# WKV recurrence of an RWKV layer on one core: quarter-array matmuls, four stores a pair, split rows for w and u, zero matmuls in pauses

## The chip, the core and the metric

The kernel runs on one core of a Trainium2 chip. The metric is the device time of one execution in microseconds; before the change the median of three runs is 369.63 us (368.87 to 372.65). The engines are named as in the profile: PE (TensorE; PEld is its weight load), DVE (VectorE), ACT (ScalarE), POOL (GpSimd) and SP (SyncE, which here only issues transfers).

## What is computed

The inputs are k and v (16 sequences of 2,048 steps by 256 channels, f32) and two vectors of 256, w and u. Each sequence and channel has a running numerator, a running denominator and a running maximum:

```python
for t in range(seq_len):
    ww = u + kk
    qq = np.maximum(pp, ww)
    e1 = np.exp(pp - qq); e2 = np.exp(ww - qq)
    output[b, t, :] = (e1 * aa + e2 * vv) / (e1 * bb + e2 + 1e-08)
    ww = pp - w + kk
    qq = np.maximum(ww, kk)
    e1 = np.exp(ww - qq); e2 = np.exp(kk - qq)
    aa = e1 * aa + e2 * vv
    bb = e1 * bb + e2
    pp = qq
```

So every step is weighted by exp(k), a state decays by exp(-w) a step, and the current step has the bonus u.

## The kernel before

**Tiling.** Time is cut into 16 chunks of 128 steps, each of two halves of 64 (`HS`). The 16 sequences are taken four at a time. One such piece (128 steps x 4 sequences x 256 channels, 512 KB) is called a pair in the code, numbered n = 4 * chunk + group; there are 64. On the chip the 128 steps are the partitions, and a tile has 128 x 1024 elements, seen as [128, 2, 512].

**One pair.** `load_k` and `load_v` (lines 61 and 66) bring 512 KB each. `round_k` (164) casts k for TensorE on DVE. `logs` (178) forms two exponents in the four PSUM banks of X: a small matmul of rows of w and u (tile `WU`, one or two rows at partitions 0, 32, 64 and 96) with coefficients `CO`, then a matmul of k with `NLE` or `NLZ`. `exps` (190) takes exp on ACT into the bf16 ring `EZR` (12 pairs). `cast_v` (197) makes v bf16, `times_v` (202) multiplies on DVE, so the ring holds four quarters: two for the denominator (0 and 1), two for the numerator (2 and 3). Ten pairs later (`LAG`) `den` (317) sums along time: matrix L (lower triangle with ones, zero between the two halves) times quarter 0, plus the identity times quarter 1, over the full 128 x 128 array, two column halves of 512 each: four matmuls of 128x512. `num` (331) does the same with LN and IdN. `recip` (325) forms 1/den on ACT as exp(-ln). `mult` (338) multiplies on DVE and stores the pair with one transfer of 512 KB from SP.

**The state.** Once a chunk, `sums` (224; 32 matmuls of 32 columns by 256), `copy_sums`, `turn` (242), `copy_turn`, `state_logs`, `state_shift`, `state_frames`, `state_offsets`, `state_weights`, `state_chain`, `state_spread`, `turn_back` (297) and `inject` (303) carry the states of all 16 sequences from half to half on PE, DVE, ACT and POOL. `inject` writes the states into rows 63 and 127 of the chunk's ring entries with four small transfers of 8 KB, so that den and num pick them up. den of a chunk's first pair needs them.

**Order.** The order is written out by hand: `keep_in_program_order` fixes it, and the loop from line 370 is one slot n per turn (76 slots). In a slot: exps(n), mult(n-11), logs(n+1), round_k(n+2), recip(n-10), den(n-9), num(n-10), times_v(n), cast_v(n+1), loads. The dictionary `later` (344) places each state step at a slot and at a place in it. Loads are issued from SP for the first 16 pairs and from POOL after that; stores and, from the third chunk on, the rows of `inject` come from SP. X takes four PSUM banks, den two and num two, each with one buffer; `num`'s banks also serve the state's matmuls. In the first nine pairs (`HALVES`) den's banks are a third buffer for the exponents (`X2`).

Of the kernel before, what the change touches and what calls it, by code (L numbers as in the profile page):

```python
# [7 lines left out]
F32 = mybir.dt.float32  # L8
F32R = mybir.dt.float32r
BF16 = mybir.dt.bfloat16  # L10
ALU = mybir.AluOpType
# [4 lines left out]
def kernel(  # L16
# [9 lines left out]
    K = tc.keep_in_program_order  # L26
    PE, DVE, SC, POOL, SP = nc.tensor, nc.vector, nc.scalar, nc.gpsimd, nc.sync

    B, T, Dm = k.shape
    HS = 64  # L30
    TC = 2 * HS
    NST = T // TC
    D = 2 * Dm
    NP = 4 * NST
    RING = 12
    LAG = 10
    FIRST = 16
    HALVES = 9
# [5 lines left out]
    consts = ctx.enter_context(tc.tile_pool(name="consts", bufs=1))  # L44
# [7 lines left out]
    psd = ctx.enter_context(tc.tile_pool(name="psd", bufs=1, space=bass.MemoryType.PSUM))  # L52
# [4 lines left out]
    def rows_of(x, n):  # L57
        c, p = divmod(n, 4)
        return x[4 * p:4 * p + 4, c * TC:(c + 1) * TC, :].rearrange("n t d -> t n d")

    def load_k(n, q):
        kr = kpool.tile([128, 4, Dm], F32, tag="kr", name="kr")
        K(q.dma_start(out=kr, in_=rows_of(k, n)))  # L63
        kr_of[n] = kr

    def load_v(n, q):
        vr = vpool.tile([128, 4, Dm], F32, tag="vr", name="vr")
        K(q.dma_start(out=vr, in_=rows_of(v, n)))  # L68
        vr_of[n] = vr


    wuf = consts.tile([128, 2, Dm], F32, tag="wuf", name="wuf")

    def rows_wu(q, x, g0):
        q = K(q.dma_start(out=wuf[g0::32, :, :], in_=bass.AP(
            tensor=x.tensor, offset=x.offset, ap=[[0, (128 - g0 + 31) // 32], [0, 2], list(x.ap[0])])))

    rows_wu(SC, w, 0)
    load_k(0, SP)
    rows_wu(SP, u, 65)  # L80
    load_k(1, SP)
    for n in range(NBUF - 1):
        load_v(n, SP)
# [3 lines left out]
    Z = consts.tile([128, D], BF16, tag="Z", name="Z")  # L87
# [9 lines left out]
    GE, NE = ALU.is_ge, ALU.not_equal  # L97

    def select(ap, cmp, fill, base, cm, pattern):
        K(POOL.affine_select(out=ap, in_=ap, pattern=pattern, compare_op=cmp,  # L100
                             fill=fill, base=base, channel_multiplier=cm))

    def matrix(name, dt):
        return consts.tile([128, 128], dt, tag=name, name=name)
# [6 lines left out]
    COf = matrix("COf", F32)  # L111
    for h in range(2):
        K(POOL.iota(COf[HS * h:HS * h + HS, :], pattern=[[0, 2], [1, HS]], base=-HS // 2 - h, channel_multiplier=0,
                    allow_small_or_imprecise_dtypes=True))
    for g in (2, 3):
        select(COf, NE, 1.0, -32 * g - 1, 1, [[0, 128]])

    NLE, NLZ, CO = matrix("NLE", F32R), matrix("NLZ", F32R), matrix("CO", F32R)
    K(DVE.tensor_scalar(NLE, M1, 0.5, None, ALU.add))
    for h in range(2):  # L120
        fill(NLE[HS * h:HS * h + HS, HS * (1 - h):HS * (2 - h)], 0.0)
    K(DVE.tensor_tensor(NLZ, NLE, I1, ALU.add))
    K(DVE.tensor_copy(CO, COf))
    WU = consts.tile([128, D], F32R, tag="WU", name="WU")
    for g, r in ((0, 1), (32, 1), (64, 2), (96, 2)):
        K(DVE.tensor_copy(WU[g:g + r, :], wuf[g:g + r].rearrange("p n d -> p (n d)")))

    mats = {}

# [30 lines left out]
    def ez(n):  # L160
        return EZR[:, :, n % RING]
# [5 lines left out]
        KM[n] = km  # L167

    X = psx.tile([128, 2, 2, D], F32, tag="X", name="X")
    X2 = psd.tile([128, 2, D], F32, tag="den", name="X2")  # L170

    def part_of(n, q):
        if n >= HALVES:
            return X[:, q]
        j = (2 * n + q) % 3
        return X2 if j == 2 else X[:, j]

    def logs(n, qs=(0, 1)):
        km = KM[n].rearrange("p (i n) d -> p i (n d)", i=2)
        for q in qs:  # L180
            for i in range(2):
                g = 32 * (2 * q + i)
                K(PE.matmul(part_of(n, q)[:, i, :], CO[g:g + 1 + q, :], WU[g:g + 1 + q, :], start=True, stop=False,  # L183
                            tile_position=(g, 0), skip_group_check=True))
        for q in qs:
            for i in range(2):
                K(PE.matmul(part_of(n, q)[:, i, :], (NLE, NLZ)[q], km[:, i, :], start=False, stop=True,  # L187
                            skip_group_check=True))
# [8 lines left out]
    def cast_v(n, eng):  # L197
        vb = vbpool.tile([128, 4, Dm], BF16, tag="vb", name="vb")
        K(eng.tensor_copy(vb, vr_of.pop(n)))  # L199
        VB[n] = vb  # L200

    def times_v(n):
        vb = VB.pop(n).rearrange("p (i n) d -> p i (n d)", i=2)
        K(DVE.tensor_mul(ez(n)[:, 2:4], ez(n)[:, 0:2], vb.unsqueeze(1).broadcast_to([128, 2, 2, D])))  # L204
# [98 lines left out]
    def inject(c):  # L303
        cb = small.tile([128, 128], BF16, tag="cb", name="cb")
        K(DVE.tensor_copy(cb, st.pop((c, "CT"))))  # L305
        r0 = 4 * c % RING
        for q in (1, 0):
            for h in range(2):
                r, x = HS * h + HS - 1, 32 * (2 * q + h)
                K((POOL if c < 2 else SP).dma_start(  # L310
                    out=EZR[r:r + 1, 2 * (1 - q), r0:r0 + 4, :, :].rearrange("o p i (b x) -> o (p i b) x", b=4),
                    in_=cb[x:x + 32, :]))


    DEN, RD, NUM = {}, {}, {}

    def den(n):
        d = psd.tile([128, 2, D], F32, tag="den", name="den")
        for m, q in (("L", 0), ("Id", 1)):
            for i in range(2):  # L320
                K(PE.matmul(d[:, i, :], mats[m], ez(n)[:, q, i, :], start=q == 0, stop=q == 1,  # L321
                            skip_group_check=True))
        DEN[n] = d

    def recip(n):
        rd = rpool.tile([128, 2, D], F32, tag="rd", name="rd")
        K(SC.activation(rd, DEN.pop(n), ACT.Ln, scale=RS))  # L327
        K(SC.activation(rd, rd, ACT.Exp, scale=-1.0))  # L328
        RD[n] = rd

    def num(n):
        d = psn.tile([128, 2, D], F32, tag="num", name="num")
        for m, q in (("LN", 2), ("IdN", 3)):
            for i in range(2):
                K(PE.matmul(d[:, i, :], mats[m], ez(n)[:, q, i, :], start=q == 2, stop=q == 3, skip_group_check=True))  # L335
        NUM[n] = d

    def mult(n):
        o = opool.tile([128, 4, Dm], F32, tag="ot", name="ot")
        K(DVE.tensor_mul(o.rearrange("p (i n) d -> p i (n d)", i=2), NUM.pop(n), RD.pop(n)))  # L340
        K(SP.dma_start(out=rows_of(out, n), in_=o))

    later = {}
    for c in range(NST):
        s = 4 * c + 3
        for slot, where, f in ((s + 1, "pe", sums), (s + 1, "dve", copy_sums),
                               (s + 2, "pe", turn), (s + 2, "dve", copy_turn),
                               (s + 3, "act", state_logs), (s + 3, "act", state_shift), (s + 3, "dve0", state_frames),
                               (s + 3, "dve0", state_offsets),
                               (s + 4, "act", state_weights), (s + 4, "dve", state_chain), (s + 4, "dve", state_spread),  # L350
                               (s + 4, "pe1", turn_back), (s + 4, "dve1", inject),
                               (s + 4, "end", state_keep)):
            later.setdefault((slot, where), []).append((f, c))

    def small_work(n, where):
        for f, c in later.pop((n, where), []):
            f(c)

    round_k(0)
    logs(0, (0,))  # L360
    logs(0, (1,))
    load_k(NBUF, SP)
    load_v(NBUF - 1, SP)
# [6 lines left out]
    for n in range(NP + LAG + 2):  # L370
        q = n - LAG
        if n < NP:
            exps(n)
        small_work(n, "act")
        if 0 <= q - 1 < NP:
            mult(q - 1)
        if n + 1 < HALVES:
            logs(n + 1, (0,))
            logs(n + 1, (1,))
        elif n + 1 < NP:  # L380
            logs(n + 1)
        small_work(n, "dve0")
        if n + 2 < NP:
            round_k(n + 2)
        small_work(n, "pe")
        small_work(n, "dve")
        if 0 <= q < NP:
            recip(q)
        if 0 <= q + 1 < NP:
            den(q + 1)  # L390
        small_work(n, "pe1")
        small_work(n, "dve1")
        if 0 <= q < NP:
            num(q)
        if n < NP:
            times_v(n)
        if n + 1 < NP:
            cast_v(n + 1, DVE if n < LAG else POOL)
        m = n + 1 + NBUF
        if m + 1 < NP:  # L400
            load_k(m + 1, SP if m + 1 < FIRST else POOL)
        if m < NP:
            load_v(m, SP if m < FIRST else POOL)
        small_work(n, "end")
        if n == 2:
            out_matrices()
# [32 lines left out]
```

## Time and profile before

| | |
|---|---|
| runs | 372.65, 368.87, 369.63 us |
| profiled execution | 367.2 us, span 365.5 us |
| mean granted clock of TensorE | 0.844 |
| busy: PE, DVE, ACT, POOL | 304.1, 257.4, 257.6, 196.3 us |
| HBM read, written | 67.12 MB, 33.55 MB |
| exp of a pair (ACT L195, 128x2048) | 1.87 us |
| ln and exp for 1/den (ACT L327, L328) | 1.02 and 1.06 us |
| cast of k, product with v, final product (DVE L166, L204, L340) | 0.87, 1.24, 1.22 us |
| issue of a k load, a v load on POOL (L63, L68) | 0.83, 0.83 us |
| issue of a store on SP (L341), of a row transfer on SP (L310) | 0.37, 0.54 us |
| store, from issue to landing | 5.4 us median, 2.9 to 10.6 |
| from one final product (DVE L340) to the next, between 60 and 290 us | 3.8 to 7.5 us |

In the profile the span is cut into 40 slices of 9.1 us; a digit is the busy share of a slice in tenths. PEclk is the granted clock of TensorE in tenths. DMA is the mean busy share of the 16 DMA engines. Stages between two times give busy time by engine, and in the timeline each line has its start, its length and what released it. A line number names the place in the kernel.

### The profile page before, as it was taken

What the parts mean: (1) busy time and instruction counts of PE and PEld (TensorE: products, weight loads), DVE (VectorE), ACT (ScalarE), POOL (GpSimd) and SP (SyncE); (2) the same over time, 40 slices, a digit from 0 to 9 for tenths busy, and PEclk for the clock granted to TensorE, in tenths of its full rate; (3) what the DMA queues carried; (4) which work ended last, traced back from release to release, by engine and by line L of the source; (5) the groups of instructions that cost most, each with busy time, mean ns of one, the idle gap of its engine ahead of it and who ended that gap; (6) DMA issues with size and microseconds to landing.
All of it is one profiled execution on the core that took longest, in us unless ns stands there. A gap on an engine that the chain in (4) does not pass through costs nothing.

```text
span 365.5 us, 4884 instructions
## 1 busy us (share of the span) xinstructions
PE 304.1 (83%) x1674; PEld 143.6 (39%) x1674; DVE 257.4 (70%) x355; ACT 257.6 (70%) x234; POOL 196.3 (54%) x279
## 2 busy tenths in 40 slices
PE   7789797969799696987989697988969788976682
PEld 2335353535344243443435253444425343533230
DVE  4773867878857757588866887575686889883652
ACT  1553558879758677679768797576775789993782
POOL 2700457887837738477764677575465745250100
PEclk9556658999859679699958997695887999998997
DMA  7999998899998979989998999889797995242465
GB/s 222 354 348 348 351 341 254 281 372 300 355 314 246 316 238 319 298 255 318 336 318 256 344 315 352 284 275 296 257 317 244 324 308 177 77 159 95 143 223 179
DMA packets 67498, 101.52 MB, mean 278 GB/s; under 512 B 5894, under 2 KB 55186, under 8 KB 67474
## 3 DMA queue, kind: packets, MB, share of 16 engines
q0 software_dynamic: 14080, 50.40, 43.2%
q1 hardware_dynamic: 53382, 50.80, 42.2%
q8 instruction: 13, 0.21, 0.2%
q14 instruction: 11, 0.09, 0.1%
q10 hardware_dynamic: 12, 0.01, 0.0%
HBM read 67.12 MB, written 33.55 MB: 275 GB/s over the span
## 4 chain that ended last, share of the span: by engine, by line
PE 62%; DVE 20%; POOL 6%; ACT 5%; issue 3%; DMA 2%; SPq 0%; DVEq 0%; POOLq 0%; ACTq 0%
PE X L187 17%; PE num L335 15%; PE den L321 13%; PE X L183 7%; DVE ot L340 7%; PE tot L231 6%; DVE km L166 4%; DVE EZR L204 4%; ACT rd L327 3%; PE TS L246 2%; PE CT L300 2%; DVE AB L284 2%; DMA vr<-in_v_dram 2%; ACT EZR L193 2%; POOL U L271 2%
## 5 line engine op out<-in xcount | busy, mean ns | idle before, releaser
L195 ACT ACTIVATE EZR<-X 128x2048 bf16<-128x2048 f32 x55 | 102.7, 1868 | 32.3 <-PE X L187 32.3
L340 DVE TENSOR_TENSOR ot<-num,rd 128x1024 f32<-128x1024 f32 x64 | 78.2, 1222 | 30.5 <-ACT rd L327 10.5
L199 POOL CAST vb<-vr 128x1024 bf16<-128x1024 f32 x53 | 55.0, 1038 | 83.1 <-DVE EZR L204 83.1
L204 DVE TENSOR_TENSOR EZR<-EZR,vb 128x2048 bf16<-128x2048 bf16 x64 | 79.5, 1241 | 2.1 <-ACT EZR L193 1.9
L327 ACT ACTIVATE rd<-den 128x1024 f32<-128x1024 f32 x64 | 65.1, 1017 | 16.6 <-PE den L321 13.9
L328 ACT ACTIVATE rd<-rd 128x1024 f32<-128x1024 f32 x64 | 67.8, 1059 | 2.0
L321 PE MATMUL den<-EZR,L 128*128 128x512 bf16 x128 | 42.4, 416 | 22.6 <-ACT rd L327 22.2
L166 DVE CAST km<-kr 128x1024 fp32r<-128x1024 f32 x64 | 55.5, 867 | 2.4 <-PE X L187 1.9
L187 PE MATMUL X<-km,NLE 128*128 128x512 f32 x128 | 54.1, 508 | 1.8 <-DVE km L166 0.9
L183 PE MATMUL X<-WU,CO 1*128 1x512 f32 (+1 forms) x256 | 42.8, 563 | 10.0 <-ACT EZR L195 5.8
L335 PE MATMUL num<-EZR,LN 128*128 128x512 bf16 x128 | 41.9, 412 | 8.7 <-DVE cb L305 5.7
L187 PE MATMUL X<-km,NLZ 128*128 128x512 f32 x128 | 47.8, 459 | 0.0
L68 POOL DMA_DIRECT2D vr<-in_v_dram x48 | 40.0, 832 | 5.0 <-DVE vb L199 4.2
L321 PE MATMUL den<-EZR,Id 128*128 128x512 bf16 x128 | 41.4, 407 | 0.0
L335 PE MATMUL num<-EZR,IdN 128*128 128x512 bf16 x128 | 41.3, 406 | 0.0
L63 POOL DMA_DIRECT2D kr<-in_k_dram x48 | 39.9, 830 | 0.0
L183 PEld LDWEIGHTS X<-WU,CO 1*128 1x128 f32 (+1 forms) x256 | 15.9, 205 | 47.2 <-issue 16.6
L193 ACT ACTIVATE EZR<-X 128x1024 bf16<-128x1024 f32 x18 | 17.9, 1022 | 20.2 <-PE X L187 20.1
L187 PEld LDWEIGHTS X<-km,NLZ 128*128 128x128 f32 x128 | 27.1, 219 | 9.2 <-issue 3.4
L187 PEld LDWEIGHTS X<-km,NLE 128*128 128x128 f32 x128 | 22.0, 215 | 20.3 <-issue 16.1
L239 DVE COPY ts<-tot 128x256 f32<-128x256 f32 x16 | 6.8, 425 | 32.2 <-PE tot L231 32.2
L231 PE MATMUL tot<-EZR,OH 128*32 128x256 bf16 x512 | 25.3, 364 | 1.4 <-DVE ot L340 1.4
(60 smaller groups left out, 233.3 us busy)
## 6 DMA issues: line engine op xcount, KB each, us to landing
out_dram<-ot SPq DMA_DIRECT2D x64, 512.0 KB, 5.4
kr<-in_k_dram POOLq DMA_DIRECT2D x48, 512.0 KB, 6.2
vr<-in_v_dram POOLq DMA_DIRECT2D x48, 512.0 KB, 7.3
kr<-in_k_dram SPq DMA_DIRECT2D x16, 512.0 KB, 8.8
vr<-in_v_dram SPq DMA_DIRECT2D x16, 512.0 KB, 8.7
EZR<-cb SPq DMA_DIRECT2D x56, 8.0 KB, 4.6
EZR<-cb POOLq DMA_DIRECT2D x8, 8.0 KB, 5.0
wuf<-in_w_dram ACTq DMA_DIRECT2D x1, 8.0 KB
```

The lines of the kernel that those rows point to most:

```text
L166: K(DVE.tensor_copy(km, kr_of.pop(n)))
L183: K(PE.matmul(part_of(n, q)[:, i, :], CO[g:g + 1 + q, :], WU[g:g + 1 + q, :], start=True, stop=False, tile_position=(g, 0), skip_group_che ...
L187: K(PE.matmul(part_of(n, q)[:, i, :], (NLE, NLZ)[q], km[:, i, :], start=False, stop=True, skip_group_check=True))
L195: K(SC.activation(ez(n)[:, 0:2], X, ACT.Exp))
L199: K(eng.tensor_copy(vb, vr_of.pop(n)))
L204: K(DVE.tensor_mul(ez(n)[:, 2:4], ez(n)[:, 0:2], vb.unsqueeze(1).broadcast_to([128, 2, 2, D])))
L231: K(PE.matmul(t[32 * j:32 * j + 32, :], mats["OH"][:, s:s + 32], ez(4 * c + p)[:, 2 * q, i, 256 * x:256 * x + 256], start=p == 0 and x == ...
L321: K(PE.matmul(d[:, i, :], mats[m], ez(n)[:, q, i, :], start=q == 0, stop=q == 1, skip_group_check=True))
L327: K(SC.activation(rd, DEN.pop(n), ACT.Ln, scale=RS))
L328: K(SC.activation(rd, rd, ACT.Exp, scale=-1.0))
L335: K(PE.matmul(d[:, i, :], mats[m], ez(n)[:, q, i, :], start=q == 2, stop=q == 3, skip_group_check=True))
L340: K(DVE.tensor_mul(o.rearrange("p (i n) d -> p i (n d)", i=2), NUM.pop(n), RD.pop(n)))
```

## The change

- `den` and `num` no longer use the full array. The function `quarters` gives, for each of the two matrices, four matmuls of 64x64 by 512: one for each time half h and each column half i, at array position (64 h, 64 i). The result has another layout: partitions are 64 i + step, and the two banks are the time halves.
- So a pair's output tile holds two sequences along the partitions, and `mult` stores it with four transfers of 128 KB, one for each h and b; on the memory side each is [2 sequences, 64 steps, 256].
- w and u go to TensorE as two bf16 rows each (`WH`, and `WU` = the value less its bf16 part where `part` is -1); `CO` is bf16. Four transfers, two on ACT and two on POOL, load w and u after a memset of `wuf`.
- State steps stand elsewhere: `sums` and `turn` come before `logs` in their slot, the state's DVE chain before `round_k`, `state_logs` and `state_weights` a slot earlier and after `recip`, `turn_back` and `inject` before `den`. `times_v` comes before `num`.
- `keep_going` adds matmuls of zeros (128x512): into den's banks, six a slot in seven of the first nine slots; after that three or six a slot, accumulated onto the next den, up to slot 62. They number 288. `X2` is gone.
- k is always loaded from SP; v from POOL from pair 16 on, as before. Of `inject`'s four rows two go from POOL and two from SP.

```diff
-    rows_wu(SC, w, 0)
     load_k(0, SP)
-    rows_wu(SP, u, 65)
+    rows_wu(SC, w, 0)
+    rows_wu(SC, w, 1)
+    rows_wu(POOL, u, 66)
+    rows_wu(POOL, u, 67)
...
-                K((POOL if c < 2 else SP).dma_start(
+                K((POOL if q == 1 else SP).dma_start(
...
-        for m, q in (("L", 0), ("Id", 1)):
-            for i in range(2):
-                K(PE.matmul(d[:, i, :], mats[m], ez(n)[:, q, i, :], start=q == 0, stop=q == 1,
-                            skip_group_check=True))
+        quarters(d, n, (("L", 0), ("Id", 1)))
         DEN[n] = d
+
+    def quarters(d, n, parts):
+        for m, q in parts:
+            for h in range(2):
+                for i in range(2):
+                    r, x = HS * h, HS * i
+                    K(PE.matmul(d[x:x + HS, h, :], mats[m][r:r + HS, r:r + HS], ez(n)[r:r + HS, q, i, :],
+                                start=q == parts[0][1], stop=q == parts[1][1], tile_position=(r, x),
+                                skip_group_check=True))
+
+    def keep_going(d, count, first):
+        for j in range(count):
+            K(PE.matmul(d[:, j % 2, :], Z[:, 0:128], Z, start=first, stop=True, skip_group_check=True))
...
-        K(DVE.tensor_mul(o.rearrange("p (i n) d -> p i (n d)", i=2), NUM.pop(n), RD.pop(n)))
-        K(SP.dma_start(out=rows_of(out, n), in_=o))
+        K(DVE.tensor_mul(o.rearrange("p (h n) d -> p h (n d)", h=2), NUM.pop(n), RD.pop(n)))
+        c, p = divmod(n, 4)
+        for h in range(2):
+            for b in range(2):
+                K(SP.dma_start(out=bass.AP(tensor=out.tensor,
+                                           offset=out.offset + ((4 * p + b) * T + c * TC + h * HS) * Dm,
+                                           ap=[[2 * T * Dm, 2], [Dm, HS], [1, Dm]]),
+                               in_=o[:, 2 * h + b, :]))
...
+        if q + 1 < 0:
+            idle_den(0 if n % 4 == 3 else 6)
+        elif n + 1 < NP:
+            keep_going(DEN[q + 1], 3 if n % 4 in (0, 3) else 6, False)
         if n + 1 < NP:
             cast_v(n + 1, DVE if n < LAG else POOL)
+        small_work(n, "pool1")
         m = n + 1 + NBUF
-        if m + 1 < NP:
-            load_k(m + 1, SP if m + 1 < FIRST else POOL)
         if m < NP:
             load_v(m, SP if m < FIRST else POOL)
+        if m + 1 < NP:
+            load_k(m + 1, SP)
```

More of the change, by code (lines that the diff above doesn't have):

```diff
@@ L72 @@
     wuf = consts.tile([128, 2, Dm], F32, tag="wuf", name="wuf")
+    K(DVE.memset(wuf, 0.0))
     def rows_wu(q, x, g0):
@@ L76, in rows_wu @@
             tensor=x.tensor, offset=x.offset, ap=[[0, (128 - g0 + 31) // 32], [0, 2], list(x.ap[0])])))
+    load_k(0, SP)
     rows_wu(SC, w, 0)
-    load_k(0, SP)
-    rows_wu(SP, u, 65)
+    rows_wu(SC, w, 1)
+    rows_wu(POOL, u, 66)
+    rows_wu(POOL, u, 67)
     load_k(1, SP)
@@ L114 @@
                     allow_small_or_imprecise_dtypes=True))
-    for g in (2, 3):
-        select(COf, NE, 1.0, -32 * g - 1, 1, [[0, 128]])
-    NLE, NLZ, CO = matrix("NLE", F32R), matrix("NLZ", F32R), matrix("CO", F32R)
+    for r in (66, 67, 98, 99):
+        select(COf, NE, 1.0, -r, 1, [[0, 128]])
+    part = consts.tile([128, 1], F32, tag="part", name="part")
+    K(POOL.memset(part, 0.0))
+    for r in (1, 33, 65, 97, 67, 99):
+        select(part, NE, -1.0, -r, 1, [[0, 1]])
+    NLE, NLZ, CO = matrix("NLE", F32R), matrix("NLZ", F32R), matrix("CO", BF16)
     K(DVE.tensor_scalar(NLE, M1, 0.5, None, ALU.add))
@@ L123 @@
     K(DVE.tensor_copy(CO, COf))
-    WU = consts.tile([128, D], F32R, tag="WU", name="WU")
-    for g, r in ((0, 1), (32, 1), (64, 2), (96, 2)):
-        K(DVE.tensor_copy(WU[g:g + r, :], wuf[g:g + r].rearrange("p n d -> p (n d)")))
+    WH = consts.tile([128, D], BF16, tag="WH", name="WH")
+    WU = consts.tile([128, D], BF16, tag="WU", name="WU")
+    wul = wuf.rearrange("p n d -> p (n d)")
+    K(DVE.tensor_copy(WH, wul))
+    K(DVE.scalar_tensor_tensor(WU, WH, part, wul, op0=ALU.mult, op1=ALU.add))
     mats = {}
@@ L169 @@
     X = psx.tile([128, 2, 2, D], F32, tag="X", name="X")
-    X2 = psd.tile([128, 2, D], F32, tag="den", name="X2")
     def part_of(n, q):
[L173 to L176, printed above, removed]
+        return X[:, q]
     def logs(n, qs=(0, 1)):
@@ L182, in logs @@
                 g = 32 * (2 * q + i)
-                K(PE.matmul(part_of(n, q)[:, i, :], CO[g:g + 1 + q, :], WU[g:g + 1 + q, :], start=True, stop=False,
+                K(PE.matmul(part_of(n, q)[:, i, :], CO[g:g + 2 + 2 * q, :], WU[g:g + 2 + 2 * q, :], start=True, stop=False,
                             tile_position=(g, 0), skip_group_check=True))
@@ L332, in num @@
         d = psn.tile([128, 2, D], F32, tag="num", name="num")
-        for m, q in (("LN", 2), ("IdN", 3)):
-            for i in range(2):
-                K(PE.matmul(d[:, i, :], mats[m], ez(n)[:, q, i, :], start=q == 2, stop=q == 3, skip_group_check=True))
+        quarters(d, n, (("LN", 2), ("IdN", 3)))
         NUM[n] = d
@@ L345 @@
         s = 4 * c + 3
[L346 to L351, printed above, removed]
+        for slot, where, f in ((s + 1, "pe0", sums), (s + 1, "dve3", copy_sums),
+                               (s + 2, "pe0", turn), (s + 2, "dve1", copy_turn),
+                               (s + 2, "act", state_logs), (s + 2, "pool1", state_shift),
+                               (s + 3, "dve0", state_frames), (s + 3, "dve0", state_offsets),
+                               (s + 3, "act", state_weights),
+                               (s + 4, "dve0", state_chain), (s + 4, "dve0", state_spread),
+                               (s + 4, "pe1", turn_back), (s + 4, "dve2", inject),
                                (s + 4, "end", state_keep)):
@@ L357, in small_work, with idle_den @@
             f(c)
+    def idle_den(count):
+        if count:
+            keep_going(psd.tile([128, 2, D], F32, tag="den", name="den"), count, True)
     round_k(0)
@@ L373 @@
             exps(n)
-        small_work(n, "act")
         if 0 <= q - 1 < NP:
             mult(q - 1)
+        small_work(n, "pe0")
+        small_work(n, "dve0")
         if n + 1 < HALVES:
@@ L381 @@
             logs(n + 1)
-        small_work(n, "dve0")
         if n + 2 < NP:
             round_k(n + 2)
-        small_work(n, "pe")
-        small_work(n, "dve")
+        small_work(n, "dve1")
         if 0 <= q < NP:
             recip(q)
+        small_work(n, "act")
+        small_work(n, "pe1")
+        small_work(n, "dve2")
         if 0 <= q + 1 < NP:
             den(q + 1)
-        small_work(n, "pe1")
-        small_work(n, "dve1")
+        if n < NP:
+            times_v(n)
+        small_work(n, "dve3")
         if 0 <= q < NP:
             num(q)
-        if n < NP:
-            times_v(n)
+        if q + 1 < 0:
+            idle_den(0 if n % 4 == 3 else 6)
+        elif n + 1 < NP:
+            keep_going(DEN[q + 1], 3 if n % 4 in (0, 3) else 6, False)
         if n + 1 < NP:
             cast_v(n + 1, DVE if n < LAG else POOL)
+        small_work(n, "pool1")
         m = n + 1 + NBUF
-        if m + 1 < NP:
-            load_k(m + 1, SP if m + 1 < FIRST else POOL)
         if m < NP:
             load_v(m, SP if m < FIRST else POOL)
+        if m + 1 < NP:
+            load_k(m + 1, SP)
         small_work(n, "end")
```

## The prediction

> **What bounds the kernel now.** I read the slices first, then the stages between times, the timeline of one slot, and last the DMA queues with their packet counts.
>
> ```profile
> PEclk9556658999859679699958997695887999998997
> DMA  7999998899998979989998999889797995242465
> GB/s 222 354 348 348 351 341 254 281 372 300 355 314 246 316 238 319 298 255 318 336 318 256 344 315 352 284 275 296 257 317 244 324 308 177 77 159 95 143 223 179
> ```
>
> The clock of TensorE falls to half again and again, yet the DMA engines are eight to nine tenths busy until the loads end at about 300 us. Two stretches of four slots each (one chunk) show what the clock does:
>
> ```profile
> 204.00:222.80 18.80, 15.61 (x106) 7.83 (x105) 15.45 (x22) 15.88 (x14) 13.90 (x19) 1.00 1.00 330
> 244.90:267.90 23.00, 19.77 (x106) 9.25 (x105) 15.34 (x22) 15.88 (x14) 13.63 (x19) 0.78 0.88 273
> ```
>
> The columns are length, busy us of PE, PEld, DVE, ACT, POOL, then clock, DMA share and GB/s. The same work takes 18.80 us at the full clock and 23.00 at 0.78. At the full clock the DMA share is 1.00: the engines of the chip are balanced, and DMA is the next limit at once. In the timeline of one slot at the full clock:
>
> ```profile
> 301.62 0.59 PE L321 MATMUL den<-EZR,L 128*128 128x512 bf16 x2
> 302.05 0.59 PE L321 MATMUL den<-EZR,Id 128*128 128x512 bf16 x2
> 302.49 0.59 PE L335 MATMUL num<-EZR,LN 128*128 128x512 bf16 x2
> 314.28 1.06 PE L231 MATMUL tot<-EZR,OH 128*32 128x256 bf16 x32
> ```
>
> Two matmuls start every 0.43 us, 0.215 each. The last line has 32 matmuls of 256 columns in 1.06 us, 33 ns each where one alone streams for 107: column tiles do run beside each other, 3.2 of 4. The queues:
>
> ```profile
> DMA packets 67498, 101.52 MB, mean 278 GB/s; under 512 B 5894, under 2 KB 55186, under 8 KB 67474
> q0 software_dynamic: 14080, 50.40, 43.2%
> q1 hardware_dynamic: 53382, 50.80, 42.2%
> q10 hardware_dynamic: 12, 0.01, 0.0%
> ```
>
> These counts tell over how many engines a transfer is spread. On q1 run 96 transfers of 512 rows of 1 KB, 56 of 32 rows of 256 B, and u's one of 4 rows: 50,948 rows. The count is 53,382, so 2,434 are extra: 152 x 16 + 2. Queue q10 is w's one transfer: 8 rows, 12 packets, 4 extra. The small packets agree: 5,894 less the 1,792 rows of 256 B is 4,102 = 2,434 + 4 + 104 x 16 (q0's). So a transfer whose outermost count is 128 or 32 has 16 extra packets, w's (4 partitions) 4, and u's (2 partitions) 2: one for each engine taking part, and the outermost count caps the engines.
>
> **The change part by part.** The profiled execution took 367.2 us, its span 365.5, so 1.7 lie around; the median shown is 369.63, 2.4 above. Sums are against 367.2.
>
> *Stores (decides).* Today a store is 128 rows outermost on both sides, 16 engines, 512 KB, landing in 5.4 us. After, four stores of 128 KB have 128 partitions on the on-chip side but [2, 64, 256] on the memory side: outermost count 2, as in u's transfer. Bounds: 16 engines each (nothing changes), or two engines, the same two each time. No row has the counts 128 and 2 together. I take two, because both sides must be cut alike and u's is the only row with a count of 2; and the same two, because u's and w's rows show nothing that would move a later transfer on. Then these two engines carry 4 x 64 = 256 rows of 1 KB per pair, and their sixteenth of k and v, 64 KB. Price of one KB: 348 to 354 GB/s in the first slices over 16 engines is 46.8 ns; the best slice, 372, gives 44.0; q1's whole share (42.2% of 16 x 365.5 us for 50.80 MB) 49.7. I take 45.4, midway of the first two, since two engines have the memory nearly to themselves. Stores: 64 x 256 x 45.4 ns = 744 us. Loads still to come when the first store issues at 60 us: the first 6.5 slices of 9.1 us move 19 MB of the 67.1 read, so 48 MB, a sixteenth is 2,930 KB, 133 us. Sum: 60 + 744 + 133 + 3 for the last landing + 1.7 + 1 (head, below) = 943 us. At 44.0 it is 916, at 49.7 about 1,026.
>
> [...] By the row of today's stores alone, 16 engines, the sum would be that of the first rival.
>
> *SP's queue.* Per slot it held one store and one transfer of a state row into EZR; now four stores, one k load and half a row transfer. An EZR transfer takes 0.54 us to issue, a store 0.37: at most 4 x 0.54 + 0.44 + 0.27 = 2.9 us per slot, under the 5.2 of a slot. In the built program each of SP's transfers waits on a semaphore of the eighth before it; that was four slots, now 1.45. Behind a late store stand the k load and the row into EZR, for which den of the next chunk waits on PE. With two engines this only keeps about two pairs of stores queued, so the two engines stay busy: no price beyond the sum. With 16 engines, 1.45 slots are 6.8 us against 5.4 to land: covered by 1.4.
>
> *Quarters.* den and num lose 8 matmuls of 0.215 (1.72 us) and get 16 of 64x64, four places of the array. Bounds: all four at once 0.86, one by one 3.44. I take 1.08, by the 3.2 of 4 of the tot row: -0.64 us a slot on PE.
>
> *Zeros.* 288 matmuls of 128x512, 246 of them in 54 slots: 4.6 x 0.215 = 0.98 us per slot on PE, standing before the next CO and km matmuls, which ACT's exp waits for. Zeros do hold the clock: the ten at the start (1.26 to 5.7 us) leave the first slice at 9 tenths. Bounds -0.5 to +0.98 a slot: with the clock held, a chunk of 20.7 (mult's starts at 58.4 and 307.0, twelve chunks apart) becomes 18.8, -0.5; I take -0.5 where PE sets the pace, and nothing behind the stores.
>
> *State work moved to the front of a slot and a slot earlier.* The waits it aims at are ACT G on POOL U, 26.8 us in 15, and den on ACT rd, 22.2 in 16. At most both go, 49 us; DVE's state chain now stands ahead of its km cast, which could cost its 1.4 us x 16. I take -15, inside what DMA leaves. *k loads from POOL to SP:* POOL loses 48 x 0.83 us and gains 24 EZR issues of 0.6, off the path; EZR's q=1 half leaves SP. *w and u in two bf16 parts:* CO loads fall from 205 towards 105 ns, hidden; 0 to -0.1 a slot, 0 taken. *Head:* w and u in four transfers behind a memset, ten more small POOL operations of about 0.3 us, so WU comes 0 to 2 us later than at 6.46: +1; DMA share is 1.10 there and covers most.
>
> All parts but the stores: 12 chunks from 20.7 to what DMA allows, 6.3 MB at 350 GB/s = 17.9, is -34, plus the head: 334.
>
> **The rivals.**
> 1. *Faster: the four stores go over all engines* (or another two each time). Then DMA stays at 4.5 us a slot, and the gain above stands: 334 us, 320 at 372 GB/s, 350 if only the clock's half comes. For it: every large transfer so far used 16. Against it: u's 2 extra packets. It decides from the engine count k: per pair (512 KB / k) x 45.4 ns + 2.9 equals today's 5.2 at k = 10.
> 2. *Quarters one after the other.* 3.44 + 0.98 against 1.72 adds 2.7 us to a PE slot of 3.8, 6.5 against 5.2: about 450 us, with stores spread. Against it: the tot row.
> 3. *SP paces.* With stores spread but landing as late as the 10.6 us seen at most, 1.45 slots take 10.6, 7.3 a slot; at the median landing nothing. 365 to 470 us.
>
> **How the numbers follow.** Two engines 0.66: 943, its own range 870 (42 ns a KB) to 1,040. First rival 0.24, 320 to 350. Second 0.05. Third 0.05, most of it within 1% to slower. A measurement of this kernel tells about 1% from no change. Faster 0.25, same 0.03, slower 0.72. The two main cases lie far apart and both are needed for eight in ten: 320 to 1,040.
>
> **What would show it.** Two engines: q1 carries 256 x (128 + 2) + 64 x 528 + 16 x 528 + 32 x 48 = 77,056 packets; sixteen would make it 80,640. The mean DMA share falls to about 0.3, GB/s to about 107, stores land after 10 us and more, ot on DVE waits for them, and PEclk stands at half. Steps on PE: 16 matmuls of den and num in about 1.1 us at the full clock; POOL issues no kr. If stores land in some 5 us and GB/s stays above 300, the forecast is wrong at its first step, and 334 is what is left.

## The result, and the profile after

The changed kernel takes 884.10 us (median of four runs, 883.17 to 888.64) where the kernel before took 369.29: a ratio of 2.392, 95% interval 2.375 to 2.408. The forecast was 943 for the likeliest case, with 870 to 1,040 as that case's own range. The profiled execution has a span of 881.9 us.

The slices of the page after, 22 us each, answer to those shown of the kernel before:

```profile
PEclk7999576665756657557575575656677565555555
DMA  9994342342433434334333244333331111111111
GB/s 306 348 282 155 112 132 92 132 129 94 133 99 124 133 95 129 129 95 133 114 110 133 90 133 128 97 133 106 117 112 49 50 49 50 49 50 49 48 48 43
```

After the first three slices the DMA engines are only three to four tenths busy, and in the last ten slices, where nothing but stores is left, one tenth. The kernel before had seven to nine tenths in every slice until its loads ended. Stages between two times give the share to two places (columns: length, busy us of PE, PEld, DVE, ACT, POOL, then clock, DMA share, GB/s):

```profile
100.00:300.00 200.00, 97.31 (x582) 41.73 (x582) 53.30 (x72) 59.09 (x51) 40.49 (x57) 0.64 0.37 118
...
640.00:800.00 160.00, 63.05 (x452) 26.81 (x444) 37.83 (x53) 45.68 (x43) 20.17 (x33) 0.61 0.17 58
800.00:881.00 81.00, 6.41 (x48) 2.08 (x48) 6.12 (x5) 6.24 (x6) 0.00 (x0) 0.50 0.13 48
```

The last stage holds stores alone, at a share of 0.13. Two engines of 16 that work without pause are 0.125, so 14 stand still. The two move 48 to 50 GB/s, 24 to 25 each. The queues after:

```profile
q1 hardware_dynamic: 77056, 75.77, 26.4%
q0 software_dynamic: 8000, 25.44, 9.3%
```

The forecast had named 77,056 packets on q1 for two engines a store and 80,640 for sixteen. Next, what the engines wait for, the longest in total (us, times, longest), and one place of the timeline:

```profile
DVE ot L352 <- DMA out_dram<-ot: 562.1, 61, 11.6
POOL vb L203 <- DVE EZR L208: 261.5, 25, 12.8
POOL EZR L314 <- DVE cb L309: 161.7, 16, 12.3
ACT EZR L199 <- PE X L191: 158.0, 35, 11.3
```

```profile
411.96 10.81 SPq L356 DMA_DIRECT2D out_dram<-ot  x4
...
418.53 1.22 DVE L352 TENSOR_TENSOR ot<-num,rd 128x1024 f32<-128x1024 f32 x1 [10.21 <-DMA out_dram<-ot]
```

The final product of a pair writes one of three tiles `ot` and can start only when the stores of three pairs ago have landed. It waits for that 61 times of 64. The other lines follow from it: POOL waits for DVE, and ACT for a PE that is itself held up by DVE. The chain that ended last says the same, before and after:

```profile
PE 62%; DVE 20%; POOL 6%; ACT 5%; issue 3%; DMA 2%; SPq 0%; DVEq 0%; POOLq 0%; ACTq 0%
```

```profile
SPq 56%; DMA 23%; DVE 8%; PE 4%; issue 3%; ACT 2%; POOL 0%; DVEq 0%; ACTq 0%; POOLq 0%
```

That the two engines are the same two each time is seen in the trace's single packets. SP issued a k load at 409.27 us. By the packet counts it closes with 16 small packets, read here as one an engine, and 14 small packets come between 415.6 and 415.9 us. The final product in the line above waited until 418.53 for stores that SP had issued before that load, and stores close with two packets each, every 2.7 us where nothing else runs. So, by this reading, 14 engines were done with a later transfer while an older store had not landed: the stores did not run on them.

From one final product to the next it takes 13.5 us while loads run, and 10.9 after the last load. 10.9 us for 256 rows of 1 KB is 42.6 ns a row on each of the two engines.

### The profile page after: what moved, and what is told of

It reads as the page before. It is cut to its first block, busy times and chain, and to the rows that moved or that the text cites. A ratio compares the mean times of both kernels' runs of the same rounds, so it can differ in the third digit from the quotient of the medians.

```text
span 881.9 us, 6781 instructions
## 1 busy us (share of the span) xinstructions
PE 396.3 (45%) x2474; PEld 169.4 (19%) x2474; DVE 243.3 (28%) x354; ACT 261.8 (30%) x234; POOL 167.3 (19%) x266
## 2 busy tenths in 40 slices
DMA packets 85113, 101.65 MB, mean 115 GB/s; under 512 B 4676, under 2 KB 78932, under 8 KB 85080
## 3 DMA queue, kind: packets, MB, share of 16 engines
q1 hardware_dynamic: 77056, 75.77, 26.4%
## 4 chain that ended last, share of the span: by engine, by line
SPq 56%; DMA 23%; DVE 8%; PE 4%; issue 3%; ACT 2%; POOL 0%; DVEq 0%; ACTq 0%; POOLq 0%
SPq L356 44%; DMA out_dram<-ot 22%; SPq L63 7%; SPq L314 5%; DVE ot L352 3%; DVE EZR L208 2%; PE X L191 2%; ACT EZR L197 2%; PE CT L304 1%; DVE AB L288 1%; PE X L187 1%; DVE CB L293 1%; DMA wuf<-in_w_dram 1%; ACT EZR L199 0%; PE TS L250 0%
## 5 line engine op out<-in xcount | busy, mean ns | idle before, releaser
L337 PE MATMUL den<-Z 128*128 128x512 bf16 x288 | 100.3, 493 | 0.0
L331 PE MATMUL num<-EZR,LN 64*64 64x512 bf16 x256 | 37.4, 572 | 106.0 <-DVE ot L352 106.0
L250 PE MATMUL TS<-Sel,ts 128*128 128x96 f32 x64 | 17.1, 416 | 83.5 <-DVE ot L352 83.5
L187 PE MATMUL X<-WU,CO 2*128 2x512 bf16 (+1 forms) x256 | 36.4, 495 | 30.8 <-ACT EZR L199 20.4
L314 POOL DMA_DIRECT2D EZR<-cb x32 | 17.5, 548 | 161.9 <-DVE cb L309 161.7
L235 PEld LDWEIGHTS <-OH 128*32 128x32 bf16 x512 | 19.6, 130 | 121.9 <-issue 119.2
L337 PEld LDWEIGHTS <-Z 128*128 128x128 bf16 x288 | 28.2, 116 | 71.4 <-issue 61.4
L331 PE MATMUL num<-EZR,IdN 64*64 64x512 bf16 x256 | 37.2, 559 | 0.0
L331 PEld LDWEIGHTS <-LN 64*64 64x64 bf16 x256 | 12.8, 145 | 125.9 <-issue 71.1
L331 PE MATMUL den<-EZR,L 64*64 64x512 bf16 x256 | 36.2, 554 | 0.7 <-ACT rd L341 0.6
```

Of the source, the lines that this page charges most:

```text
L314: K((POOL if q == 1 else SP).dma_start(out=EZR[r:r + 1, 2 * (1 - q), r0:r0 + 4, :, :].rearrange("o p i (b x) -> o (p i b) x", b=4), in_=cb ...
L331: K(PE.matmul(d[x:x + HS, h, :], mats[m][r:r + HS, r:r + HS], ez(n)[r:r + HS, q, i, :], start=q == parts[0][1], stop=q == parts[1][1], til ...
L337: K(PE.matmul(d[:, j % 2, :], Z[:, 0:128], Z, start=first, stop=True, skip_group_check=True))
```

## The experiments

Theory, the author's assumption, which the runs below try: the number of engines is the largest up to 16 that divides the outermost counts of both sides of a transfer. It fits the small packets of the kernel before (2 for a count of 2, 4 for 4, 16 for 32 and 128) and the changed kernel's q1, 77,056 packets, which has 2 a store for 128 with 2. By it two engines carry each new store, and by the single packets above the same two each time. Rivals: the number of stores and SP's issuing cost the time; or quarters, zeros or the new order do.

**e1_spread** gives the four stores another cut: the same bytes, rows, number and queue, but 64 outermost on both sides.

```diff
         for h in range(2):
-            for b in range(2):
+            for i in range(2):
                 K(SP.dma_start(out=bass.AP(tensor=out.tensor,
-                                           offset=out.offset + ((4 * p + b) * T + c * TC + h * HS) * Dm,
-                                           ap=[[2 * T * Dm, 2], [Dm, HS], [1, Dm]]),
-                               in_=o[:, 2 * h + b, :]))
+                                           offset=out.offset + ((4 * p + 2 * i) * T + c * TC + h * HS) * Dm,
+                                           ap=[[Dm, HS], [T * Dm, 2], [1, Dm]]),
+                               in_=o[HS * i:HS * i + HS, 2 * h:2 * h + 2, :]))
```

> The changed kernel with one edit: the four stores of a pair are cut by time half and array column half (64 rows of 64 partitions on both sides, two sequences each) in place of time half and sequence, so the outermost count is 64 on both sides instead of 128 and 2. Bytes, row size (1 KB), number of stores, queue and order are the same. Two-engine theory: 16 engines share each store, the hardware queue carries 80,640 packets, stores land in 3 to 7 us, the time is 320 to 350 us (first rival of the prediction, 334). Rival (it is the number of stores and SP's issue of 2.6 us each that cost, not the engines): SP still needs 4 x 2.6 us a pair and the time stays above 800 us.

Measured: 348.21 us (346.84 to 349.78), a ratio of 0.941 to the kernel before, interval 0.936 to 0.945. Of its page, the slices, q1, and the landing of stores:

```profile
DMA  8999989999999999999999999999999975557797
...
q1 hardware_dynamic: 80640, 75.78, 72.0%
...
out_dram<-ot SPq DMA_DIRECT2D x256, 128.0 KB, 5.4
```

The changed kernel and this one lie 536 us apart and differ in these four lines only, so the whole loss hangs on the access pattern, and the rest of the change is worth having. The packets are the 80,640 named for 16 engines. The rival of store count and issuing falls: SP issues as many stores, now 0.61 us each (median) instead of 2.63. Nor was it the old pattern that was dear to issue. The k load (L63), whose pattern is the same in both kernels, also took longer to issue in the changed kernel, 2.45 us against 0.58 (durations in ns, least, median and most; the changed kernel first, then e1):

```profile
L63 SPq DMA_DIRECT2D kr<-in_k_dram x64: 367/2448/3853, 0.8 to 653.6; - x64
L356 SPq DMA_DIRECT2D out_dram<-ot x256: 565/2628/4293, 60.5 to 869.9; - x128
```

```profile
L63 SPq DMA_DIRECT2D kr<-in_k_dram x64: 368/578/1868, 0.8 to 268.8; - x64
L356 SPq DMA_DIRECT2D out_dram<-ot x256: 595/607/1546, 60.6 to 341.4; - x128
```

**e2_before_cut122** leaves everything as before the change and cuts the one store of a pair in two.

```diff
-        K(SP.dma_start(out=rows_of(out, n), in_=o))
+        for x, y in ((0, 122), (122, 128)):
+            K(SP.dma_start(out=rows_of(out, n)[x:y], in_=o[x:y]))
```

> The kernel before with one edit: the store of a pair is cut at row 122 into two stores of 122 and 6 rows of partitions. Two-engine theory, by its divisor form: 122 has no divisor up to 16 above 2, so two engines carry 61 x 4 rows of 1 KB each, and six engines 4 rows each of the other; the busiest engine has 248 rows a pair, 64 x 248 x 42 ns = 667 us (42 ns: 49 GB/s over two engines in the last 250 us of the changed kernel), with 60 us before the first store and some 130 of loads about 860 us. The hardware queue carries 52,598 packets: 53,382 less 64 x 16 plus 64 x (2 + 6) is 52,870 if extra packets count engines. Rival (only counts of sequences on the memory side matter, or the quarters and the new order do): within 3% of 369 us.

Measured: 858.04 us (one run) beside 370.99. (Of the two packet counts in the expectation the second, 52,870, is the one its sum gives.)

```profile
q1 hardware_dynamic: 52870, 50.80, 17.8%
```

So an innocent-looking row count slows the old kernel about as much as the change did. No quarters, zeros or new order are needed. Both sides count 122 here, so a low count on the memory side is not needed; a common divisor fits this run (2 and 6 small packets a pair) and the changed kernel (2 a store).

**e9, e10, e11** move the cut, and so the number of engines: `(0, 124)`, `(0, 119)`, `(0, 121)` in place of `(0, 122)`.

> The kernel before with its store cut at row 124: 124 and 4 rows. The engine count that divides 124 is 4. Theory (busiest engine sets the pace): 31 x 4 + 4 = 128 rows of 1 KB a pair, at 42 ns 344 us for 64 pairs, plus 60 us before the first store, 123 for a sixteenth of the loads still to come, 5 around: about 530 us. Rival (the loss comes from two engines in particular, or from having two stores): 860 as for the cut at 122, or 370.

> The kernel before with its store cut at row 119: 119 and 9 rows, 7 engines for the first and 9 for the second. Theory: 17 x 4 + 4 = 72 rows on the busiest engines, 3.0 us a pair, with 2.7 of loads 5.7 us against the 5.2 of a pair today, so the engines just begin to decide: 375 to 400 us.

> The kernel before with its store cut at row 121: 121 and 7 rows, 11 engines and 7. Theory: 11 x 4 + 4 = 48 rows on the busiest engines, 2.0 us a pair, with 2.7 of loads 4.7, under the 5.2 of a pair: 366 to 378 us. The prediction put the turning point at 10 engines.

| cut at | engines by the divisor | rows of 1 KB a pair on the busiest | expected us | measured us |
|---|---|---|---|---|
| none | 16 | 32 | | 370.3 |
| 121 | 11 (and 7) | 48 | 366 to 378 | 374.15, ratio 1.012 (1.005 to 1.019) |
| 119 | 7 (and 9) | 72 | 375 to 400 | 413.20, ratio 1.111 (1.100 to 1.123) |
| 124 | 4 (and 4) | 128 | 530 | 543.77 (one run) |
| 122 | 2 (and 6) | 248 | 860 | 858.04 (one run) |

The time follows the rows on the busiest engine, and the packets on q1 agree with the divisor: 53,510 at 121, where each pair has 11 + 7 extra ones, 53,382 at 119 (7 + 9), 52,870 at 124 (4 + 4). The count gives only the sum of a pair's two stores; the last ten and the last eight slices, where stores alone run, tell 122 from 124: 46 to 52 GB/s against 81 to 96. All four cut kernels have two stores a pair, and at 121 they cost 1%, so having two stores is not the loss.

```profile
q1 hardware_dynamic: 53510, 50.80, 43.6%
```

The turning point lies between 7 engines (ratio 1.111) and 11 (1.012), as the prediction's 10. At 119 the upper end of the expectation was 13 us short. A wait that the sum leaves out is on that page: den waits 27.1 us for the state rows of `inject`, which SP issues behind the stores (PE den on DMA EZR<-cb). The kernel before has no such wait among its longer ones. That it makes up the 13 us was not tried apart.

**e3_pool_stores** issues the stores of the changed kernel, uncut, from POOL (`K(SP.dma_start` becomes `K(POOL.dma_start`).

> The changed kernel with its stores as they are (outermost counts 128 and 2) issued by POOL instead of SP. It asks whether the two engines are the same two for each transfer. If the choice is the same on POOL's path: about 880 us. If POOL's path takes the next engines in turn: the load evens out, and POOL's own issuing (304 transfers of 0.55 to 0.8 us, 200 us, beside 55 us of casts) decides: 340 to 430 us. If POOL's path spreads each over 16: the same 340 to 430, with 16 extra small packets per store instead of 2.

Measured: 552.36 us (one run), in none of the ranges expected.

```profile
GB/s 283 348 348 287 251 246 189 166 253 196 251 154 240 166 237 181 194 229 150 253 177 239 180 235 185 216 220 194 212 180 105 85 78 89 73 84 73 93 76 36
DMA packets 121464, 102.58 MB, mean 186 GB/s; under 512 B 65604, under 2 KB 107092, under 8 KB 121432
...
out_dram<-ot POOLq DMA_DIRECT2D x256, 128.0 KB, 10.7
```

In the last slices stores alone move 73 to 93 GB/s, more than the 50 of two engines, so on POOL's queue it is not the same two for every store. What holds it at 552 was not shown by a run. An estimate: POOL's issue of a store waits for earlier stores to land (77.7 us in 51 waits), by the program for the transfer eight earlier, and a store lands only 10.7 us after its issue. POOL's queue has 5.25 transfers a slot here, so eight are 1.5 slots and a slot takes 7.0 us: 450 us for 64, 510 with the 60 before the first store. The other 40 us are not accounted for; POOL's state steps and casts now stand behind its waiting stores, which wasn't tried apart.

**e4, e5, e6, e7, e8, e12** ask what the other parts are worth once the stores are spread.

e4 takes all zero matmuls out of e1; e8 leaves about half:

```diff
-            keep_going(DEN[q + 1], 3 if n % 4 in (0, 3) else 6, False)
+            keep_going(DEN[q + 1], 2 if n % 4 in (0, 3) else 3, False)
```

> The kernel of e1_spread without its 288 zero matmuls (nothing of the result is left out). The prediction's step: the zeros hold the clock, worth about 2 us a chunk of four pairs, so without them 350 to 370 us at a mean clock of 0.80 to 0.88. Rival (they only stand before the next pair's matmuls): 5 to 15 us faster than e1_spread.

> The kernel of e1_spread with two or three zeros a slot in place of three or six, from the tenth slot on. Theory (the clock is held by how busy PE is, and falls when too few are left): between 348 and the 380 to 405 without zeros, 355 to 385, at a mean clock of 0.82 to 0.93. Rival (half of them hold it, and the rest only stand in the way): 340 to 347 us at 0.95.

Measured: e8 359.31 us, ratio 0.970 (0.961 to 0.978), inside the theory's range. e4 took 379.93 us once (clock 0.81) and 404 to 407 three times (0.70 to 0.78), all above the 350 to 370 expected. With one run so far from the others no ratio is given; even this best run is 32 us above e1. The clocks, e1 first, then e4 in its run of 406.69 us:

```profile
PEclk9589999999999999999999899999999999999885
```

```profile
PEclk9999997697667956696668898666959597665595
```

The mean clock is 0.944 to 0.960 in e1's runs, 0.88 to 0.91 in e8's, 0.81 in e4's best run, and 0.83 to 0.87 in the runs of the kernel before beside it. So the fewer zeros, the lower the clock and the longer the time, and without them nothing is left of the gain: e4's best run is slower than the 370.99 of the kernel before. Why three of its four runs are slower still is not shown.

e5 takes the quarters out of e1 and keeps the zeros (den and num as before, one store of 512 KB a pair). e6 adds 246 zeros to the kernel before and nothing else:

```diff
         if n < NP:
             times_v(n)
+        if q + 1 >= 0 and n + 1 < NP:
+            keep_going(DEN[q + 1], 3 if n % 4 in (0, 3) else 6, False)
```

> The kernel of e1_spread with den and num on the full array again (four matmuls of 128x512 each) and, as the layout then allows, one store a pair; zeros, order of the state, k on SP stay. In e1_spread four slots take 18.7 us at the full clock, as the best chunks of the kernel before do. Theory (the quarters buy PE time that the zeros use): each slot has 0.6 to 0.9 us more on PE, 21 to 22 us a chunk, 375 to 395 us in all. Rival (PE has room, DMA sets the pace at 330 GB/s): 344 to 352 us.

> The kernel before with the zero matmuls alone, from the slot of the first den on (246 of the 288), behind times_v. Theory (the loss of the kernel before is the clock): the clock rises to 0.95 or more from 60 us on and twelve chunks of 20.7 us become 18.8, 342 to 350 us. Rival (PE is full: 4.6 zeros of 0.215 us a slot lengthen every slot of 3.8 to 4.7 by 0.98): four slots take 22 to 23 us, 375 to 395 us.

Measured: e5 373.97 us, ratio 1.011 (1.004 to 1.017), a microsecond under its theory's range; e6 361.85, ratio 0.978 (0.972 to 0.985), between its theory and its rival. One chunk of four slots of e1, e5 and e6, all at the full clock; the mean of twelve chunks is the same to 0.1 us:

```profile
228.90:247.70 18.80, 16.17 (x155) 7.76 (x154) 14.63 (x20) 15.90 (x14) 11.92 (x17) 1.00 0.99 322
```

```profile
226.90:247.60 20.70, 18.61 (x122) 9.37 (x123) 14.44 (x20) 16.11 (x15) 12.25 (x17) 1.00 0.94 302
```

```profile
221.10:241.10 20.00, 19.04 (x122) 9.56 (x122) 15.46 (x21) 15.92 (x15) 13.58 (x19) 1.00 0.95 309
```

Zeros alone hold the clock but fill PE (19.04 of 20.00 us), so a chunk stays at 20.0 and the gain is 8 us. Quarters, with the four stores that go with them, make room for the zeros: 18.8 against e5's 20.7, and 348 in all against 374. Quarters without zeros gain nothing (e4). In e1's timeline the quarters are seen at work:

```profile
238.18 0.41 PE L331 MATMUL den<-EZR,L 64*64 64x512 bf16 x4
238.42 0.39 PE L331 MATMUL den<-EZR,Id 64*64 64x512 bf16 x4
238.64 0.39 PE L331 MATMUL num<-EZR,LN 64*64 64x512 bf16 x4
238.85 0.39 PE L331 MATMUL num<-EZR,IdN 64*64 64x512 bf16 x4
239.17 0.82 PE L337 MATMUL den<-Z 128*128 128x512 bf16 x3
```

Four matmuls start about every 0.215 us where before there was one: all four places of the array run together.

e7 loads k from POOL again, from pair 16 on (`load_k(m + 1, SP if m + 1 < FIRST else POOL)`); e12 goes the other way and loads all v from SP too (`load_v(m, SP)`).

> The kernel of e1_spread with k loaded from POOL from pair 16 on, as before the change. POOL's queue moves 4 KB in a packet, SP's 1 KB. Theory (the DMA engines set the pace at a share of 0.9 to 1.0): time per byte falls a little and SP's queue is shorter, 338 to 346 us. Rival (POOL's 40 us more of issuing delays its cast of v and state steps): 348 to 358 us. Within 1% of 348 if the queue doesn't matter.

> The kernel of e1_spread with all v loads from SP too. Moving k from SP back to POOL cost 6.7 us, so the same step with v could gain as much, 340 to 346 us, if POOL's issuing is what it cost. Rival (packets of 1 KB and SP's queue, which now holds six transfers a slot with 0.65 us each): 350 to 365 us.

Measured: e7 354.94 us, ratio 0.960 (0.952 to 0.967); e12 368.70, ratio 0.994 (0.989 to 0.999). So k on SP is worth 7 us, and e7's rival came in: in the chain of its page POOL has 38%, in e1's 8%. v on SP costs 20, more than even e12's rival had. In e12 the final product waits 39.8 us for stores to land, in e1 2.1. SP holds 6.5 transfers a slot there, and by the program each waits for the eighth before it; whether this queue or the packets of 1 KB cost more was not separated.

e1_spread is the fastest of all the kernels: 348.21 us against 369.29 before and 884.10 after.

## Why the prediction was right

*Stores: engine count.* Right as it stood: two engines, with the packet count exact (77,056). The inference from u's two and w's four extra packets held for unlike counts (128 and 2). That both sides must be cut alike was the author's assumption; the runs show 2 small packets a store for 128 with 2, 16 for 64 with 64 (80,640 on q1 in e1), and packet counts and times that fit a common divisor for the four cuts, e2 and e9 to e11.

*Stores: the same two engines.* This was the weaker step, taken because no row showed a change of engines. The single packets around 415 us and the last stage (share 0.13, 48 GB/s) show it true of SP's queue; e3 shows that it is not true of POOL's. So the step was right for the queue that the change uses, by a choice and not by evidence.

*Stores: the price of a row.* Mis-sized: 45.4 ns taken, 42.6 measured. 64 x 256 x 2.8 ns is 46 us of the 59 between 943 and 884. The loads make up the rest: 2.6 us a pair for 45 pairs is 117 instead of 133, 16 less, and some 3 go the other way. The measured price lies under every price that the prediction took from a row (44.0 to 49.7). Its own range reached below 884 only by 42 ns a KB, which it took from no row; its sum at 42 is 877, not the 870 written. So the size was met with some luck. That two engines have the memory nearly to themselves was its reason, and no run tests it.

*SP's queue.* No price beyond the sum was right, but 0.54 us at most for an issue was wrong: a store took 2.63 and a k load, with its pattern unchanged, 2.45. The four issues at 411.96 us lasted 10.81, about the 10.9 that the rows of a pair take on the two engines; in e1, with stores landing in 5.4 us, a store took 0.61 and a k load 0.58. So the issues went at the pace of the stores and did not set it; what lengthens them was not shown.

*Quarters.* 1.08 us a slot was taken on the strength of 3.2 of 4; e1's four groups, one every 0.215 us, are 0.86, the lower bound. The 3.2 came from a row of 1.06 us that includes the end of its last matmul. In the rows of den, two matmuls last 0.59 us where two starts take 0.43. Less this 0.16 the 32 matmuls take 28 ns each, by this estimate 3.8 of 4.

*Zeros.* That they hold the clock was right (e6: nine tenths or more in the seventh to the 37th slice, 54 to 334 us, and 1.00 in the chunk above, where the kernel before has 0.85 from 60 to 290). That a chunk then takes 18.8, -0.5 us a slot, was wrong for zeros alone by their own cost: 20.0, or -0.2. It takes the quarters as well to reach 18.8.

*State work.* -15 us was taken. e5 and e6 both have zeros and the full array; e5 has the new order, k on SP, split w and u, 42 more zeros at the start and no `X2` as well, and is 12 us slower. The k loads help by 7 in e1. So the rest, the new order above all, may cost some 12 to 19 us under a full PE rather than gain; nothing of it was run by itself, and the size stays open.

*k loads from POOL to SP.* They were put off the path, at nothing. Moving them back costs 7 us (e7).

*First rival.* Its mechanism (stores spread) was tried in e1: 348 against the 334 it gave, near the upper end of its 320 to 350. The step that was too hopeful is a chunk at 17.9 us by DMA alone; it takes 18.8 at a share of 0.99 and 322 GB/s, not 350. *Second rival* (quarters one after the other) falls by the timeline above. *Third rival* (SP paces with stores landing late) did not come in: in e1 they land in 5.4 us (median; 8.6 at most), and the final product waits 2.1 us for them in all.

## What to carry to other kernels

Read a transfer's access pattern on both sides before issuing it, for a low common divisor of the outermost counts. In these runs, on SP's queue, 128 with 2 left 14 of 16 DMA engines idle for a factor of 2.4, and 122 on both sides cost about as much (858.04 us against 370.99); a divisor of 7 cost 11%, one of 11 1%, and 64 on both sides ran on 16. The profile tells it without any experiment: small packets per transfer in the queue's count (2 a store here, 16 in e1), and a DMA share near that number of sixteenths where such stores are all that runs (0.13 for two engines; two tenths in the last eight slices of e9, for four). Zeros that held the clock gained 8 us where PE was full and made the quarters pay where PE had room, so they belong together with what makes that room.

## What was not expected of the hardware

- POOL's queue does not keep to the same two engines: 73 to 93 GB/s in stores alone where SP's queue had 48 to 50. With the same stores it also sent 60,928 more packets under 512 B (65,604 in e3, 4,676 in the changed kernel), 238 a store.
- An issue of a store on SP took 2.63 us instead of 0.61 with only the access pattern changed, and a k load's 2.45 instead of 0.58 with its own pattern unchanged. Why was not shown by a run.
- With only two DMA engines at work, each moved 24 to 25 GB/s in rows of 1 KB, against 21.8 to 22.1 each when all 16 were loading (348 to 354 GB/s in early slices of the kernel before).
